# One run of narrow products for two weight units in a decoder layer

## The chip, the cores and the metric

The kernel runs on one core of a Trainium2 chip. The metric is the time of one execution on the device in microseconds (us). Three runs of the kernel before gave 642.34, 642.52 and 642.67 us; the median is 642.52.

## The reference

A decoder layer for 256 positions of width 1024, all in float32: a SwiGLU half step, a mixer of causal attention (8 heads of 128) and a short gated convolution, and a second SwiGLU half step, each followed by a layer norm.

```python
def swiglu(x, w_up, w_down):
    gate, up = jnp.split(x @ w_up, 2, axis=-1)
    return (jax.nn.silu(gate) * up) @ w_down

# one layer
x = layer_norm(ALPHA * x + 0.5 * swiglu(x, ffn1_w_up, ffn1_w_down), ln1_g, ln1_b)
z = x @ w_in                                  # (256, 8192): q, k, v, h, g_b, g_c, gates
mix = (gate_attn * (attention(q, k, v) @ w_proj_attn)
       + gate_conv * ((g_b * short_conv(g_c * h)) @ w_proj_conv)) @ w_out
x = layer_norm(ALPHA * x + mix, ln2_g, ln2_b)
x = layer_norm(ALPHA * x + 0.5 * swiglu(x, ffn2_w_up, ffn2_w_down), ln3_g, ln3_b)
```

With 256 positions the attention has a single block of keys, so it is plain causal attention. The width of the ffns is 2816.

## The kernel before

**Products.** Each float32 matrix is split into a high half, rounded to the matmul's format, and a low half, what the rounding left. A product of two matrices is high by high, high by low and low by high; low by low is left out. Weights come from memory in units of 1 MB (`Unit`, line 40): ScalarE casts a unit's `raw` buffer into the high half (tile `S`, line 895), VectorE subtracts it from the raw values into the low half (tile `LC`, or `LR` for units read by rows, line 898), in two chunks a unit (`prep`, line 889). A cast of a new unit waits until a buffer is free. `S` has five, `LC` three and `raw` three buffers; in part of the mixer two of the `S` buffers and both of `LR` hold queries and keys.

**Columns and rows.** Where the result is wanted transposed, the weights are stationary (`cols`, line 356). A unit of 1024 x 256 weights gives two blocks of 128 output columns, each with an accumulator (tile `acc`, one of eight banks). For each block and each of the eight slices `k` of the input (KT is 8) there is one *wide* product, the high weights by both halves of the input (tile `X`, 512 columns), and one *narrow* product, the low weights by the high input (256 columns). So a unit has 16 wide and 16 narrow products. A block whose last product is issued is evacuated by its epilogue, which begins with a ScalarE copy (line 386) and a VectorE addition (line 387). The order is set by hand at line 383: nine wide products, that is the eight of the first block and one of the second; the sixteen narrow ones of both blocks; the other seven wide ones. In a sequence of units the seven and the nine of the next unit form sixteen wide ones. Where the input is stationary (`rows`, `rows_both`, and `D` for the down projection), all products are 512 wide.

**Stages.** `ffn` (line 390) goes over eleven groups `j` of 256 hidden columns. The first one or two groups go by rows; each later one is `U_cols(j)`: a unit of gate weights, then one of up weights. Behind it comes `D` for group `j - 2`, 24 products for both halves of the positions, whose four accumulators stay in use until the end of the ffn. The mixer computes the values by rows, and then 14 times four blocks with `four` (line 550): q, k, q, k, the gates, h, gc, gb, each with two units. Projections `P` (line 765) do the same four times, and `O` ends the mixer by rows. In all there are 74 units with stationary weights.

**What sets the order.** TensorE's sequence is the list `base`, built in the order above. Other steps (transposes, attention's products, softmax) are put into it at planned times: `put(at, dt, ops)` inserts them `dt` us behind place `at` by a clock that counts columns / 2400 + 0.0025 us a product (line 851). A head's scores, transposes and value products are put at 1.3, 11.8 and 16.3 us behind the first keys, 7.5 us further for each head (line 747). A final loop goes over the sequence and issues everything (line 933): ahead of each product `advance` (line 910) issues what is due, loads on SyncE's queue (line 884) as raw buffers come free, casts as `S` and low buffers come free and at least 2.2 us apart, in the order in which units are first used (lines 867 to 875). A unit's buffers are given back with its last product (lines 937 to 941). The sixteen sigmoids of the gates go to ScalarE 0.6 us apart behind the first `H` (line 751).

Of the kernel before, what the change touches and what calls it, by code (L numbers as in the profile page):

```python
# [19 lines left out]
KT = DM // 128  # L20
# [45 lines left out]
def layer(ctx: ExitStack, tc: tile.TileContext, a: dict, out: bass.AP):  # L66
# [53 lines left out]
    def mm(dst, lhsT, rhs, start, stop, cols, unit=None):  # L120
        return Op(lambda: nc.tensor.matmul(dst(), lhsT=lhsT(), rhs=rhs(), start=start, stop=stop), cols, unit)  # L121

    def passes(dst, sta, mov, first, last, cols, unit=None):

        return [mm(dst, lambda x=x: sta(x), lambda w=w: mov(w), first and i == 0, last and i == 2, cols, unit)
                for i, (x, w) in enumerate(((0, 0), (0, 1), (1, 0)))]

    def add(ops):
        base.extend(ops)
        return len(base)  # L130
# [5 lines left out]
    def defer(dt, fn, unit=None):  # L136
        pending.append((now["t"] + dt, unit, fn))
# [7 lines left out]
    def new_unit(src, chunks=2, use="rows"):  # L145
        u = Unit(src, chunks, use)
        units.append(u)
        return u
# [37 lines left out]
    def col_unit(w, c0):  # L186

        return new_unit(lambda raw: [(raw.rearrange("p (k n) -> p k n", k=KT),
                                      w[:, c0:c0 + 256].rearrange("(k p) n -> p k n", p=128))], use="cols")
# [24 lines left out]
    def split_later(hi, lo, src, done=None, dt=0.8):  # L214
        def rest():
            nc.vector.tensor_tensor(lo, src, hi.bitcast(F), op=OP.subtract)
            if done:
                done()

        def first():  # L220
            nc.scalar.copy(hi, src)  # L221
            defer(0.5, rest)

        defer(dt, first)
# [128 lines left out]
            add([ops[i]])  # L353
        return len(base)

    def cols(key, u, epis):

        box, wide, narrow = {}, [], []
        for b in range(2):
            for k in range(KT):
                c = slice(k * 256 + b * 128, k * 256 + (b + 1) * 128)
                wide.append(mm(lambda b=b: box[b], lambda c=c: u.hi[:, c],
                               lambda k=k: st["xT", key][:, k].rearrange("p s t n -> p (s t n)"),
                               k == 0, b == 1 and k == KT - 1, 512, u))
                narrow.append(mm(lambda b=b: box[b][:, 0:256], lambda c=c: u.lo[:, c],
                                 lambda k=k: st["xT", key][:, k, 0].rearrange("p t n -> p (t n)"),  # L370
                                 False, b == 0 and k == KT - 1, 256, u))
        for b, end in ((0, narrow[KT - 1]), (1, wide[-1])):
            def first(b=b, f0=wide[b * KT].fn):
                box[b] = ACC.get()
                f0()

            def fin(b=b):
                epis[b](box[b])
                ACC.free()

            wide[b * KT].fn = first
            end.after.append(fin)
        return add(wide[:KT + 1] + narrow + wide[KT + 1:])

    def both(dst, bank):
        nc.scalar.copy(dst, bank[:, 256:512])  # L386
        nc.vector.tensor_tensor(dst, dst, bank[:, 0:256], op=OP.add)  # L387


    def ffn(key, wu, wd, ln_i, by_rows, order, tail, after_ln):  # L390
# [4 lines left out]
        def hT_of(j, kk):  # L395
            if ("hT", key, j, kk) not in st:
                st["hT", key, j, kk] = T.get(R).rearrange("p (s n) -> p s n", s=2)
            return st["hT", key, j, kk]
# [27 lines left out]
        def U_cols(j):  # L426
            ug, uu = col_unit(wu, j * 256), col_unit(wu, DFF + j * 256)

            def gate(bank, b):
                g = T.get()  # L430
                both(g[:, 0:256], bank)
                defer(0.8, lambda: nc.scalar.activation(g[:, 0:256], g[:, 0:256], AF.Silu))  # L432
                st["g", j, b] = g

            def up(bank, b):
                g = st["g", j, b]
                both(g[:, 256:512], bank)
                nc.vector.tensor_tensor(g[:, 0:256], g[:, 0:256], g[:, 256:512], op=OP.mult)  # L438
                hT = hT_of(j, b)
                split_later(hT[:, 0], hT[:, 1], g[:, 0:256], T.free, 1.1)  # L440

            cols(key, ug, [lambda bank, b=b: gate(bank, b) for b in range(2)])
            cols(key, uu, [lambda bank, b=b: up(bank, b) for b in range(2)])
            if j == NJ - 1:
                base[-1].after.append(X.free)

# [52 lines left out]
        for j in js:  # L499
            U_cols(j)  # L500
            while done <= j - 2:
                D([done], 0)
                if done < NJ - tail:
                    D([done], 1)
                done += 1
        e0 = D(list(range(done, NJ)), 0)
        last = list(range(NJ - tail, NJ))
# [27 lines left out]
    win = a["w_in"][0]  # L535
    COLS = {"q": 0, "k": 1024, "v": 2048, "h": 3072, "gb": 4096, "gc": 5120, "ga": 6144, "gv": 7168}

    def V(c, t):
        if ("v", c) not in st:
            st["v", c] = row_units(win, COLS["v"] + c * 512)  # L540

        def epi(bank):
            if c == 0 and t == 0:
                st["v"] = X.get(R).rearrange("p (s t n) -> p s t n", s=2, t=2)
            cs = slice(c * 512, (c + 1) * 512)
            split(st["v"][:, 0, t, cs], st["v"][:, 1, t, cs], bank)

        return rows("m", t, st["v", c], epi)

    def four(kind, c, epi):  # L550

        for p in range(2):
            u = col_unit(win, COLS[kind] + c * 512 + p * 256)
            e = cols("m", u, [lambda bank, j=p * 2 + b: epi(bank, j) for b in range(2)])
        return e

    def QK(kind, c):
        def epi(bank, j):
            if j == 0:
                state["hold" + kind] -= 1  # L560
                pool = st["pool", kind, c] = S if kind == "q" else L["rows"]
                st[kind, c] = pool.get(R).rearrange("p (s h n) -> p s h n", s=2, h=4)
            t_ = T.get()
            both(t_[:, 0:256], bank)
            split_later(st[kind, c][:, 0, j], st[kind, c][:, 1, j], t_[:, 0:256], T.free)

        return four(kind, c, epi)

    def H(c):
        def epi(bank, j):  # L570
            if j == 0:
                st["h", c] = N.get()
            both(st["h", c][:, j * 256:(j + 1) * 256], bank)

        return four("h", c, epi)

    def GC(c):
        def epi(bank, j):
            if j == 0:
                st["u", c] = N.get().rearrange("p (j n) -> p j n", j=4)  # L580
                nc.gpsimd.memset(st["u", c][:, :, 0:2], 0.0)
            u, hc, ch = st["u", c][:, j], st["h", c][:, j * 256:(j + 1) * 256], c * 4 + j
            t_ = T.get()
            both(t_[:, 0:256], bank)
            nc.vector.tensor_tensor(u[:, 2:258], t_[:, 0:256], hc, op=OP.mult)
            T.free()

            def tap2():
                nc.scalar.activation(hc, u[:, 2:258], AF.Identity, bias=cvec[:, 24 + ch:25 + ch], scale=cvec[:, 16 + ch:17 + ch])

            def taps():
                for s in (1, 0):
                    nc.vector.scalar_tensor_tensor(hc, u[:, s:s + 256], cvec[:, s * 8 + ch:s * 8 + ch + 1],
                                                   hc, op0=OP.mult, op1=OP.add)
                if j == 3:
                    N.free()

            defer(1.0, tap2)
            defer(2.6, taps)

        return four("gc", c, epi)
# [118 lines left out]
    for t in range(2):  # L720
        for c in range(2):
            e = V(c, t)
# [17 lines left out]
    for c in range(2):  # L740
        QK("q", c)
        e = QK("k", c)
# [20 lines left out]


    def P(key, w, n, epi):
        for p in range(2):
            u = col_unit(w, n * 512 + p * 256)
            cols(key, u, [lambda bank, j=p * 2 + b: epi(bank, j) for b in range(2)])

    def A_epi(n):  # L770
        def epi(bank, j):
# [22 lines left out]
    for n in range(2):  # L794
        P("a", a["w_proj_attn"][0], n, A_epi(n))
        if n == 1:
            base[-1].after.append(X.free)
        P("c", a["w_proj_conv"][0], n, C_epi(n))
# [170 lines left out]
```

## Time and profile before

| | |
|---|---|
| median of three runs | 642.52 us |
| profiled execution | 642.42 us |
| its span, first to last instruction | 640.5 us |
| TensorE's products | 3416, busy 631.6 us |
| TensorE's weight loads | 3416, busy 545.3 us |
| VectorE | busy 454.3 us |
| ScalarE | busy 355.2 us |
[...]

The profile names engines PE (TensorE's products), PEld (its weight loads), DVE (VectorE), ACT (ScalarE), POOL and SP. Products overlap each other in the array, so one product's duration is longer than the distance between two starts; the distance is read from the timeline, in which neighbours of one kind are merged into a row with the start of the first one and their number. A row's own length ends with the end of the last product, so a run's time is the start of the next row less its own start. Products read `acc<-X,S` (wide, stationary weights), `acc<-X,LC` (narrow, stationary weights), `acc<-S,T` and `acc<-LR,T` (down projection).

### The profile page before, as it was taken

What the parts mean: (1) busy time and instruction counts of PE and PEld (TensorE: products, weight loads), DVE (VectorE), ACT (ScalarE), POOL (GpSimd) and SP (SyncE); (2) the same over time, 40 slices, a digit from 0 to 9 for tenths busy, and PEclk for the clock granted to TensorE, in tenths of its full rate; (3) what the DMA queues carried; (4) which work ended last, traced back from release to release, by engine and by line L of the source; (5) the groups of instructions that cost most, each with busy time, mean ns of one, the idle gap of its engine ahead of it and who ended that gap; (6) DMA issues with size and microseconds to landing.
All of it is one profiled execution on the core that took longest, in us unless ns stands there. A gap on an engine that the chain in (4) does not pass through costs nothing.

```text
span 640.5 us, 8790 instructions
## 1 busy us (share of the span) xinstructions
PE 631.6 (99%) x3416; PEld 545.3 (85%) x3416; DVE 454.3 (71%) x732; ACT 355.2 (55%) x624; POOL 19.3 (3%) x25
## 2 busy tenths in 40 slices
PE   9999999999999999999999999999999999999995
PEld 6888888888888888898888888888888888888884
DVE  4786666666677678778768987889966666666637
ACT  5765555555533567677678664553555555555530
POOL 2000000000011000000000000001100000000001
PEclk9999999999999999999999999999999999999999
DMA  8766666557654475454646665576555755555401
GB/s 296 262 231 200 215 235 197 185 183 251 214 163 131 138 227 162 148 181 132 196 138 199 201 210 175 197 236 225 196 197 200 259 195 185 184 188 189 178 1 67
DMA packets 95854, 121.18 MB, mean 189 GB/s; under 512 B 2196, under 2 KB 84548, under 8 KB 95812
## 3 DMA queue, kind: packets, MB, share of 16 engines
q1 hardware_dynamic: 95524, 120.23, 57.2%
q8 instruction: 27, 0.44, 0.3%
q10 hardware_dynamic: 288, 0.39, 0.2%
q14 instruction: 15, 0.12, 0.1%
HBM read 119.56 MB, written 1.05 MB: 188 GB/s over the span
## 4 chain that ended last, share of the span: by engine, by line
PE 98%; DVE 1%; issue 0%; DVEq 0%; ACT 0%; POOL 0%; POOLq 0%
PE acc L121 96%; PE acc L198 2%; PE acc L155 0%; DVE N L835 0%; DVEq L965 0%; DVE LR L898 0%; DVE N L839 0%; ACT X L211 0%; POOL T L94 0%; DVE bn L248 0%; DVE N L246 0%; DVE mv L258 0%; PE acc L730 0%; DVE X L212 0%; DVEq L898 0%
## 5 line engine op out<-in xcount | busy, mean ns | idle before, releaser
L121 PE MATMUL acc<-X,S 128*128 128x512 f32 x1184 | 288.8, 392 | 0.0
L121 PEld LDWEIGHTS acc<-X,S 128*128 128x128 f32 x1184 | 216.5, 188 | 41.3
L895 ACT CAST S<-raw 128x1024 fp32r<-128x1024 f32 (+1 forms) x224 | 225.9, 1033 | 18.6 <-PE acc L121 14.4
L898 DVE TENSOR_TENSOR LC<-raw,S 128x1024 fp32r<-128x1024 f32 x166 | 201.7, 1224 | 24.9 <-ACT S L895 23.2
L121 PEld LDWEIGHTS acc<-X,LC 128*128 128x128 f32 x1184 | 149.8, 189 | 5.6
L121 PE MATMUL acc<-X,LC 128*128 128x256 f32 x1184 | 152.4, 281 | 0.0
L387 DVE TENSOR_TENSOR T<-T,acc 128x256 f32<-128x256 f32 x132 | 55.3, 419 | 97.3 <-ACT T L386 97.2
L121 PE MATMUL acc<-S,T 128*128 128x512 f32 (+1 forms) x364 | 112.1, 383 | 0.0
L386 ACT COPY T<-acc 128x256 f32<-128x256 f32 x132 | 48.9, 370 | 110.9 <-PE acc L121 110.7
L121 PEld LDWEIGHTS acc<-S,T 128*128 128x128 f32 x364 | 67.5, 188 | 13.3
L898 DVE TENSOR_TENSOR LR<-raw,S 128x1024 fp32r<-128x1024 f32 (+1 forms) x58 | 66.1, 1147 | 8.2 <-ACT S L895 8.1
L121 PE MATMUL acc<-S,X 128*128 128x512 f32 x224 | 71.6, 395 | 0.0
L121 PE MATMUL acc<-LR,T 128*128 128x512 f32 (+1 forms) x164 | 63.1, 385 | 0.0
L121 PEld LDWEIGHTS acc<-S,X 128*128 128x128 f32 x224 | 42.0, 188 | 9.5 <-ACT S L895 0.6
L121 PEld LDWEIGHTS acc<-LR,T 128*128 128x128 f32 x164 | 30.8, 188 | 6.1
L221 ACT CAST T<-T 128x256 fp32r<-128x256 f32 x38 | 15.5, 407 | 33.7 <-DVE T L438 33.7
L211 ACT CAST X<-acc 128x512 fp32r<-128x512 f32 x16 | 9.4, 586 | 26.9 <-PE acc L198 16.1
L432 ACT ACTIVATE T<-T 128x256 f32<-128x256 f32 x38 | 15.9, 418 | 14.3 <-DVE T L387 14.3
L121 PE MATMUL acc<-LC,X 128*128 128x512 f32 x56 | 22.6, 403 | 0.0
L121 PE MATMUL acc<-LR,X 128*128 128x512 f32 x56 | 22.0, 392 | 0.3 <-DVE LR L898 0.3
L212 DVE TENSOR_TENSOR X<-acc,X 128x512 fp32r<-128x512 f32 x16 | 11.0, 690 | 15.2 <-ACT X L211 15.0
L260 POOL TENSOR_TENSOR rs<-mv,mhalf 128x1 f32<-128x1 f32 x6 | 6.2, 1038 | 457.9 <-DVE mv L258 457.9
(83 smaller groups left out, 319.9 us busy)
## 6 DMA issues: line engine op xcount, KB each, us to landing
raw<-in_ffn_w_up SPq DMA_DIRECT2D x38, 1024.0 KB, 5.1
raw<-in_w_in SPq DMA_DIRECT2D x32, 1024.0 KB, 5.4
raw<-in_ffn_w_down SPq DMA_DIRECT2D x22, 1024.0 KB, 5.0
raw<-in_w_proj_attn SPq DMA_DIRECT2D x4, 1024.0 KB, 5.0
raw<-in_w_proj_conv SPq DMA_DIRECT2D x4, 1024.0 KB, 5.0
raw<-in_w_out SPq DMA_DIRECT2D x4, 1024.0 KB, 5.0
raw<-in_ffn_w_up SPq DMA_DIRECT2D x8, 512.0 KB, 5.1
raw<-in_ffn_w_up SPq DMA_DIRECT2D x8, 256.0 KB, 5.6
```

The costliest lines, as they stand in the source:

```text
L121: return Op(lambda: nc.tensor.matmul(dst(), lhsT=lhsT(), rhs=rhs(), start=start, stop=stop), cols, unit)
L198: nc.tensor.transpose(box["t"][:, i * 128:(i + 1) * 128], src(i), ident)
L211: nc.scalar.copy(hi, src)
L212: nc.vector.tensor_tensor(lo, src, hi.bitcast(F), op=OP.subtract)
L221: nc.scalar.copy(hi, src)
L260: nc.gpsimd.tensor_tensor(rs, mv[:, 1:2], mhalf, op=OP.pow)
L386: nc.scalar.copy(dst, bank[:, 256:512])
L387: nc.vector.tensor_tensor(dst, dst, bank[:, 0:256], op=OP.add)
L432: defer(0.8, lambda: nc.scalar.activation(g[:, 0:256], g[:, 0:256], AF.Silu))
L895: nc.scalar.copy(u.hi[:, s], u.raw[:, s])
L898: nc.vector.tensor_tensor(u.lo[:, s], u.raw[:, s], u.hi[:, s].bitcast(F), op=OP.subtract)
```

## The change

`cols` takes a list of units. With two of them it issues 25 wide products (all of the first unit's sixteen, eight of the second's first block and one of its second), then the 32 narrow ones of all four blocks, then the seven wide ones that are left. The epilogues of the first three blocks follow the last narrow product of each, that of the fourth the last wide one. `U_cols`, `four` and `P` hand over their two units together. The first group by columns of the first ffn (`j == by_rows`) stays as two single units. Nothing else is changed.

```diff
-    def cols(key, u, epis):
+    def cols(key, uns, epis):
         box, wide, narrow = {}, [], []
-        for b in range(2):
+        last = 2 * len(uns) - 1
+        for b in range(last + 1):
+            u = uns[b // 2]
             for k in range(KT):
-                c = slice(k * 256 + b * 128, k * 256 + (b + 1) * 128)
-                wide.append(mm(lambda b=b: box[b], lambda c=c: u.hi[:, c],
+                c = slice(k * 256 + b % 2 * 128, k * 256 + (b % 2 + 1) * 128)
+                wide.append(mm(lambda b=b: box[b], lambda c=c, u=u: u.hi[:, c],
                                lambda k=k: st["xT", key][:, k].rearrange("p s t n -> p (s t n)"),
-                               k == 0, b == 1 and k == KT - 1, 512, u))
-                narrow.append(mm(lambda b=b: box[b][:, 0:256], lambda c=c: u.lo[:, c],
+                               k == 0, b == last and k == KT - 1, 512, u))
+                narrow.append(mm(lambda b=b: box[b][:, 0:256], lambda c=c, u=u: u.lo[:, c],
                                  lambda k=k: st["xT", key][:, k, 0].rearrange("p t n -> p (t n)"),
-                                 False, b == 0 and k == KT - 1, 256, u))
-        for b, end in ((0, narrow[KT - 1]), (1, wide[-1])):
+                                 False, b < last and k == KT - 1, 256, u))
+        for b in range(last + 1):
...
-            end.after.append(fin)
-        return add(wide[:KT + 1] + narrow + wide[KT + 1:])
+            (wide[-1] if b == last else narrow[(b + 1) * KT - 1]).after.append(fin)
+        n = last * KT + 1
+        return add(wide[:n] + narrow + wide[n:])
...
-            cols(key, ug, [lambda bank, b=b: gate(bank, b) for b in range(2)])
-            cols(key, uu, [lambda bank, b=b: up(bank, b) for b in range(2)])
+            epis = [lambda bank, f=f, b=b: f(bank, b) for f in (gate, up) for b in range(2)]
+            if key == "x" and j == by_rows:
+                cols(key, [ug], epis[:2])
+                cols(key, [uu], epis[2:])
+            else:
+                cols(key, [ug, uu], epis)
...
-        for p in range(2):
-            u = col_unit(win, COLS[kind] + c * 512 + p * 256)
-            e = cols("m", u, [lambda bank, j=p * 2 + b: epi(bank, j) for b in range(2)])
-        return e
+        uns = [col_unit(win, COLS[kind] + c * 512 + p * 256) for p in range(2)]
+        return cols("m", uns, [lambda bank, j=j: epi(bank, j) for j in range(4)])
...
-        for p in range(2):
-            u = col_unit(w, n * 512 + p * 256)
-            cols(key, u, [lambda bank, j=p * 2 + b: epi(bank, j) for b in range(2)])
+        uns = [col_unit(w, n * 512 + p * 256) for p in range(2)]
+        cols(key, uns, [lambda bank, j=j: epi(bank, j) for j in range(4)])
```

## Rows read from the trace of the kernel before

**Rows 1.** The page's part 1: busy us (share of the span) xinstructions of each engine.

```profile
PE 631.6 (99%) x3416; PEld 545.3 (85%) x3416; DVE 454.3 (71%) x732; ACT 355.2 (55%) x624; POOL 19.3 (3%) x25
```

**Rows 2.** The page's part 4: the chain that ended last, by engine.

```profile
PE 98%; DVE 1%; issue 0%; DVEq 0%; ACT 0%; POOL 0%; POOLq 0%
```

**Rows 3.** Waits of the weight loads: us in total, times, longest us.

```profile
PEld acc L121 <- ACT S L895: 0.6, 1, 0.6
```

**Rows 4.** Groups of instructions: shapes xcount | busy us, mean ns | idle before.

```profile
L121 PE MATMUL acc<-X,S 128*128 128x512 f32 x1184 | 288.8, 392 | 0.0
L121 PEld LDWEIGHTS acc<-X,S 128*128 128x128 f32 x1184 | 216.5, 188 | 41.3
L121 PE MATMUL acc<-X,LC 128*128 128x256 f32 x1184 | 152.4, 281 | 0.0
L387 DVE TENSOR_TENSOR T<-T,acc 128x256 f32<-128x256 f32 x132 | 55.3, 419 | 97.3 <-ACT T L386 97.2
```

**Rows 5.** Timeline of PE, first ffn, one period (start us, us, ...).

```profile
80.36 2.20 PE L121 MATMUL acc<-X,S 128*128 128x512 f32 x9
82.40 2.05 PE L121 MATMUL acc<-X,LC 128*128 128x256 f32 x16
84.28 3.82 PE L121 MATMUL acc<-X,S 128*128 128x512 f32 x16
87.94 2.05 PE L121 MATMUL acc<-X,LC 128*128 128x256 f32 x16
89.83 1.78 PE L121 MATMUL acc<-X,S 128*128 128x512 f32 x7
91.44 0.39 PE L121 MATMUL acc<-S,T 128*128 128x512 f32 x1
...
96.88 0.62 PE L121 MATMUL acc<-X,S 128*128 128x512 f32 x2
```

**Rows 6.** Timeline of PE, first ffn: first rows of two periods, six apart.

```profile
63.84 2.20 PE L121 MATMUL acc<-X,S 128*128 128x512 f32 x9
...
162.96 2.20 PE L121 MATMUL acc<-X,S 128*128 128x512 f32 x9
```

**Rows 7.** Timeline of PE, mixer: a run of six narrow products.

```profile
266.56 0.87 PE L121 MATMUL acc<-X,LC 128*128 128x256 f32 x6
267.27 2.69 PE L121 MATMUL acc<-X,S 128*128 128x512 f32 x11
269.80 0.49 PE L198 MATMUL acc<-ident,T 128*128 128x128 f32 x3
```

**Rows 8.** Timeline of all engines, first ffn: a narrow run's loads and products.

```profile
104.24 2.06 PEld L121 LDWEIGHTS acc<-X,LC 128*128 128x128 f32 x16
104.46 2.05 PE L121 MATMUL acc<-X,LC 128*128 128x256 f32 x16
```

**Rows 9.** Timeline of PE, mixer: a narrow run behind an attention step.

```profile
304.64 1.98 PE L121 MATMUL acc<-X,LC 128*128 128x256 f32 x16
306.45 1.56 PE L121 MATMUL acc<-X,S 128*128 128x512 f32 x6
```

**Rows 10.** Timeline of PE, mixer: the rest of a narrow run behind three transposes.

```profile
298.59 1.40 PE L121 MATMUL acc<-X,LC 128*128 128x256 f32 x10
299.82 3.82 PE L121 MATMUL acc<-X,S 128*128 128x512 f32 x16
```

**Rows 11.** Timelines of PE and ACT, mixer, while the sigmoids run: a release, two casts.

```profile
330.43 3.81 PE L121 MATMUL acc<-X,S 128*128 128x512 f32 x16
...
335.57 1.04 ACT L895 CAST S<-raw 128x1024 fp32r<-128x1024 f32 x1
...
338.21 1.04 ACT L895 CAST S<-raw 128x1024 fp32r<-128x1024 f32 x1
```

**Rows 12.** DMA issues: KB each, median us from issue to landing.

```profile
raw<-in_w_in SPq DMA_DIRECT2D x32, 1024.0 KB, 5.4
```

**Rows 13.** Windows 251:318, 318:337 and 337:348 summed: us, then each engine's busy us.

```profile
sum 97.00, PE 97.00 PEld 86.28 DVE 74.28 ACT 71.67 POOL 0.11; mean PE 32.33 PEld 28.76 DVE 24.76 ACT 23.89 POOL 0.04
```

## The prediction

> **What bounds the kernel now.** I read the page's engine list first, then the chain, then the waits of TensorE, then its products in order of time. TensorE is busy 99% of the span, the next engine 71% [rows 1], and 98% of the chain that ended last is TensorE [rows 2]. Its loads waited three times for a weight in the whole span, 0.6 us at the longest [rows 3]. So no wait is left to remove: the time is the number of products times the distance from one start to the next. Busy times (392 and 281 ns for one product, [rows 4]) don't give that distance, because products overlap; I take it from the starts in the timeline.
>
> One ffn pair of units shows it [rows 5]. The first nine wide products go from 80.36 to 82.40, 2.04 us or 226.7 ns each. Sixteen narrow ones follow in 1.88 us, 117.7 ns each. Then sixteen wide ones take from 84.28 to 87.94, 3.66 us, where sixteen at 226.7 ns would take 3.63; the seven after the second narrow run take 1.61 us against 1.59. The 24 products of the down projection are back at 226.7 ns (91.44 to 96.88, 5.44 us). So wide products behind a narrow run start slow and recover: each return from narrow to wide costs about 30 ns; the step from wide to narrow costs nothing that I can see. Six such periods, from 63.84 to 162.96 [rows 6], take 99.12 us, 16.52 each; 56 wide ones at 226.7 and 32 narrow ones at 117.7 ns would be 16.46. The 0.06 us left belong to two narrow runs: **30 ns a run**, now at a resolution of a few ns.
>
> **What the change removes.** There are 1184 wide and 1184 narrow products with stationary weights [rows 4], 16 of each in a unit: 74 units, 37 pairs. The first pair of the first ffn stays as it is, 36 pairs are merged, and each loses one narrow run. 36 x 0.030 = **1.1 us**. Products, loads and columns stay the same in number, and so do all instructions of the other engines and all DMAs.
>
> Does a run of 32 return to wide products more dearly than one of 16? A run of only six narrow ones (266.56 to 267.27) is followed by eleven wide ones in 2.53 us, 0.03 over eleven at 226.7 [rows 7]: the same 30 ns as behind sixteen. The cost is one of the return, not of the run's length, so I take 30 ns behind 32 too. The bounds are 60 ns, twice the cost behind twice the run, which leaves a gain of nothing, and 0, which would make it 36 x 0.060 = 2.2 us; [rows 7] speak for the middle.
>
> Is the second half of a longer run as fast as the first? The loads of a narrow run start at 104.24 and take 2.06 us, its products start at 104.46 and take 2.05 [rows 8]: the loads stay one product ahead from first to last, and no reserve is being used up. [...] A bound on the other side: where an attention step broke the rhythm, sixteen narrow ones took from 304.64 to 306.45, 1.81 us, 113 ns each [rows 9]. If the second half of each long run fell into that rhythm, 36 x 16 x 0.0045 = 2.6 us more would be gained. Nothing in the sixteen places of an undisturbed run moves that way, so I take 117.7.
>
> **What it moves.** Attention steps are put at planned times in the sequence and now meet other products. A step's three transposes cost the run that they break little: the ten narrow products behind them take 1.23 us where 1.18 is due [rows 10]; other steps leave the faster rhythm of [rows 9] behind, 0.07 us a run the other way. By the planner's own clock two of the eight fall into narrow runs, about as now. I count 0 and +-0.2 us.
>
> The epilogues of three of the four blocks come 8 narrow products apart (0.94 us) after the change, no longer spread over the pair; the last stays at the pair's end. Four accumulators are open instead of two. In the ffns the down projection holds four more, so all eight are in use, but its 24 products (5.44 us, [rows 5]) stand between two pairs and cover the last epilogue, an addition of 0.42 us [rows 4] behind a copy. In the mixer the other four are free. Cost 0; without that cover a pair would wait about 0.8 us, an estimate that takes the copy to be as long as the addition.
>
> The weights are held longer. Now a unit's buffers come free 5.54 us after its first product; after the change the first unit's come free behind 25 wide and 16 narrow ones, 25 x 0.2267 + 16 x 0.1177 = 7.55 us into the pair, the second's at its end, 11.05. With three buffers for low halves the first unit of the next pair is cast from the start of this pair and gains time. The second one is cast from 7.55 us on, and its first wide product is due at 11.05 + 16 x 0.2267 + 0.03 = 14.7: **7.15 us** instead of two units, 11.1. Where ScalarE is free its two casts, planned 2.2 us apart, have room; where it is late it is close. The latest I find is among the sigmoids: the unit released at about 332.0 (seven products into the run of 330.43) was followed by casts at 335.57 and 338.21 to 339.25, 7.25 us [rows 11]. That would be 0.1 us too late after the change, but the second cast is needed only four wide products later, 0.9 us: 0.8 us is left. DMA issues on SyncE keep their order and move with the releases; a load needs 5.4 us [rows 12], and its raw buffer is free from the cast three units earlier, over a pair's 11 us ahead. The low halves are needed later than now, behind 25 or more wide products, which covers VectorE's lag.
>
> **The sum.** The profiled execution took 642.42 us, its span 640.5; the median of the runs is 642.52, so a difference of the span carries over. 642.5 - 1.1 = **641.4**, 640.5 - 1.1 = 639.4 for the span.
>
> **Rivals.**
> - *No gain* (642.5): the 30 ns are no price of the return, but follow the number of narrow products before it, or come back elsewhere. For it: the excess is small beside the rounding of one row. Against it: six periods agree, and six narrow ones cost as much as sixteen [rows 6, 7]. [...]
> - *A wait for weights at one or two places* (641.6 to 642.5): the second unit of a pair comes late behind the sixteen sigmoids of ScalarE, near 335 to 341, where 0.8 us is left. Each us beyond that is one us of TensorE, once.
> - *Slower* (646 to 647): the same wait over the whole stretch from 251 to 348, where ScalarE is busy 71.7 of 97 us [rows 13]. It decides from the point where ScalarE is over 4.3 us late to a release (3.5 is the worst here). About nine pairs lie there; at 5 us late each loses 0.7, 6 us in all, less the 1.1 gained: 647. Against it: in that stretch epilogues and casts are the same work, only in other bursts.
> - *More gain* (638.8): the faster rhythm of [rows 9] in the second halves.
>
> **How the numbers follow.** Forecast 641.4 +-0.3: 0.66. Wait at one or two places 0.10, no gain 0.09, slower 0.07, more gain 0.08. What a measurement can tell is about 0.2%, 1.28 us: the forecast of 1.1 lies just inside it, and a third of its 0.66, for the steps that are moved and for the bound of the return, lies beyond, 0.22. Faster 0.22 + 0.08 = 0.30; same 0.44 + 0.10 + 0.09 = 0.63; slower 0.07. The range runs from 640.3, where the return is free behind 32 (2.2 us), to 642.7; it takes in the forecast, the single wait and no gain, and leaves out 0.15.
>
> **What would show it.** In the ffns of the changed kernel a period should be 25 wide ones in 5.67 us, 32 narrow ones in 3.77 without a step at the seventeenth, seven wide ones in 1.61, and 16.49 us in all against 16.52. The wide run in the middle of the pair must show no slow start. The rows of waits of TensorE's loads should hold no new entry for ScalarE's casts; one near 341 would be the single wait, entries at each pair from 251 on the slower case. Casts of a pair should come as two and two, the second pair of casts some 7.6 us into it. I am wrong if the seven wide ones behind 32 take over 1.64 us, if narrow ones drift, or if loads wait.

## The result and the profile after

The changed kernel takes 648.2 us (648.07 to 648.97) beside 642.55 us for the kernel before: a ratio of 1.0091, 95% interval 1.0079 to 1.0103. It is 5.6 us slower where 1.1 us less was forecast, and it lies outside the range. The execution profiled took 648.07 us, its span is 646.3 us against 640.5 us, so the 5.8 us can be looked for in the trace.

The page's engine list and its chain by engine, after:

```profile
PE 633.1 (98%) x3416; PEld 544.5 (84%) x3416; DVE 452.3 (70%) x732; ACT 351.1 (54%) x624; POOL 19.9 (3%) x25
PE 86%; DVE 9%; ACT 4%; issue 1%; DVEq 0%; POOL 0%; ACTq 0%; POOLq 0%
```

The engine list hardly differs from [rows 1]: the instructions are the same in number, and VectorE and ScalarE are even a little less busy. The share of TensorE falls by one point, too little to draw the eye. The chain is what changed: 98% TensorE in [rows 2], now 86%, with 13% on VectorE and ScalarE. The waits of the weight loads say at what it stands (engine, line, what is waited for: us in total, times, longest us):

```profile
PEld acc L121 <- DVE T L212: 3.5, 5, 2.2
PEld acc L121 <- DVE LR L902: 2.4, 3, 1.2
PEld acc L121 <- DVE LC L902: 2.0, 2, 1.2
...
PEld acc L121 <- ACT X L221: 0.7, 1, 0.7
PEld acc L121 <- ACT S L899: 0.6, 1, 0.6
```

The wait for ScalarE's cast is what it was (0.6 us, [rows 3]). New is the wait for the attention's transposed probabilities (`T`, line 212), and so is one for the input of `O` (`X`, line 221). The waits for low halves of weights (`LR` and `LC`, line 902) have grown: in the kernel before there was one of each, 0.6 and 0.3 us. What is new lies in two stretches. In the windows of the kernel after, then of the kernel before (length in us, busy us and number of instructions of each engine, granted clock, DMA share, GB/s), 225 to 310 us is queries, keys and the first attention steps, 425 to 475 us the end of the mixer and the first rows of the second ffn:

```profile
225.00:310.00 85.00, 83.00 (x492) 72.44 (x491) 64.32 (x145) 57.07 (x131) 0.00 (x0) 1.00 0.49 149
...
425.00:475.00 50.00, 47.45 (x221) 37.72 (x221) 42.39 (x64) 24.00 (x36) 6.04 (x4) 1.00 0.61 202
```

```profile
225.00:310.00 85.00, 85.00 (x514) 75.50 (x513) 67.34 (x155) 59.00 (x138) 0.00 (x0) 1.00 0.57 171
...
425.00:475.00 50.00, 50.00 (x231) 40.76 (x230) 41.59 (x61) 25.15 (x37) 6.04 (x4) 1.00 0.66 215
```

TensorE issues 22 products fewer in the one and ten fewer in the other, at a granted clock of 1.00 in both kernels (over the whole span 0.998 before, 0.996 after): it is not the clock. No engine is busier there than before, but for VectorE in the second window, by 0.8 us. What is lost is lost by waiting.

For the place to a few hundredths of a us I take the start of each stage's first product from TensorE's timeline (inside a merged row by its place in the row) and compare stage lengths with those of the kernel before. The columns of the table: the attention part is from the second queries (`q1`) to `gc0`, eight pairs, then `O`, then the rows of the second ffn's first group, and the rest are the stages in which only the length of undisturbed work can change. The rows below the first belong to the experiments. (The rest of m_mid and of v_c0a1c1 holds 0.3 us that lie ahead of the first merged pair, where the program is the same.)

| kernel | attention part | `O` | first rows of ffn 2 | all the rest | span |
|---|---|---|---|---|---|
| after | +3.10 | +2.1 | +1.6 | -1.1 | +5.8 |
| e_hold | +1.6 | +1.4 | +1.6 | +0.1 | +4.7 |
| e_late | +1.6 | -0.2 | 0.0 | 0.0 | +1.4 |
| e_both | +1.1 | 0.0 | +1.6 | +0.1 | +2.8 |
| e_ffn | 0.0 | 0.0 | 0.0 | -0.7 | -0.7 |
| m_tail | +3.1 | 0.0 | +1.6 | -1.1 | +3.6 |
| m_attn | +1.8 | +2.1 | +1.6 | -1.2 | +4.3 |
| m_mid | +1.7 | -0.1 | +1.6 | -1.4 | +1.9 |
| m_at2 | +0.1 | +2.1 | +1.6 | -1.2 | +2.7 |
| b_at2 | +0.2 | 0.0 | 0.0 | 0.0 | +0.2 |
| b_cast77 | 0.0 | 0.0 | +1.6 | 0.0 | +1.7 |
| v_c0a1c1 | +0.1 | 0.0 | 0.0 | -1.3 | -1.2 |
| v_p21 | +0.1 | +1.1 | 0.0 | -1.1 | +0.1 |

So the gain that was forecast is there, -1.1 us outside the disturbed stages, and three losses stand against it: 3.1 + 2.1 + 1.6 = 6.8 us. The 2.1 us of `O` are two things: 0.6 in its first quarter, the wait for its own input (`X`), and 1.5 in its second, waits for low halves.

**The gain.** The same period of the first ffn as in [rows 5] (start us, us, engine, line, what), and, from the view of all engines, the weight loads of its narrow run:

```profile
80.25 5.83 PE L121 MATMUL acc<-X,S 128*128 128x512 f32 x25
85.69 3.95 PEld L121 LDWEIGHTS acc<-X,LC 128*128 128x128 f32 x32
85.92 3.93 PE L121 MATMUL acc<-X,LC 128*128 128x256 f32 x32
89.69 1.77 PE L121 MATMUL acc<-X,S 128*128 128x512 f32 x7
91.30 0.39 PE L121 MATMUL acc<-S,T 128*128 128x512 f32 x1
...
96.74 0.62 PE L121 MATMUL acc<-X,S 128*128 128x512 f32 x2
```

25 wide products in 5.67 us (226.8 ns each, no slow start in the middle), 32 narrow ones in 3.77 (117.8 ns), seven wide ones in 1.61, the period 16.49 us against 16.52. All four are the forecast's numbers. The loads of the 32 take 3.95 us, their products 3.93 us: they stay one product ahead from first to last.

**Where the attention's loss shows first.** ScalarE, at the first keys' pair of units (`k0`; last bracket: idle before, and what ended it):

```profile
228.26 1.05 ACT L899 CAST S<-raw 128x1024 fp32r<-128x1024 f32 x1
232.35 0.37 ACT L389 COPY T<-acc 128x256 f32<-128x256 f32 x1 [3.04 <-PE acc L121]
```

The copy is the first step of the pair's first epilogue. It used to be due behind nine wide and eight narrow products, now it is due behind 25 and eight: 16 x 0.2267 = 3.6 us later (in the traces it starts at 229.17 us before and at 232.35 after). ScalarE stands 3.04 us, and then three epilogues fall due 0.94 us apart (their copies start at 232.35, 233.52 and 235.04 us). From this instant on the chain that ended last has no piece of TensorE for 55 us, only ScalarE and VectorE (start us, us, what; the pieces between are casts, copies, subtractions and softmax steps):

```profile
214.43 17.89 PE acc L121 x97
...
232.35 0.38 ACT T L389
...
286.72 0.30 DVE T L212
287.06 4.30 PE acc L121 x27
```

TensorE feels it first at the second head's value products. After, then before:

```profile
259.98 0.49 PE L198 MATMUL acc<-ident,T 128*128 128x128 f32 x3
264.96 0.37 ACT L211 CAST T<-acc 128x256 fp32r<-128x256 f32 x1
266.33 0.42 DVE L212 TENSOR_TENSOR T<-acc,T 128x256 fp32r<-128x256 f32 x1
266.80 0.19 PEld L121 LDWEIGHTS acc<-T,X 128*128 128x128 f32 x1 [2.18 <-DVE T L212]
```

```profile
260.44 0.49 PE L198 MATMUL acc<-ident,T 128*128 128x128 f32 x3
262.89 0.37 ACT L211 CAST T<-acc 128x256 fp32r<-128x256 f32 x1
264.11 0.29 DVE L212 TENSOR_TENSOR T<-acc,T 128x128 fp32r<-128x128 f32 x1 [0.33 <-ACT T L211]
265.40 0.70 PE L121 MATMUL acc<-T,X 128*128 128x512 f32 x4
```

Before, ScalarE takes the transposed probabilities 2.45 us behind the transposes, and VectorE ends its second split (264.40) 1.0 us ahead of the products. After, ScalarE comes 4.98 us behind the transposes, the first split ends at 266.75, and the load behind it starts at once, at 266.80. The products had been put there by the planned clock, and TensorE starts nothing of what stands behind them in its list either: its loads stand for 2.18 us, its products for 1.75. ScalarE does nothing for 3.04 us here and 3.39 us below, each time ahead of a copy whose product was still to come.

**The end of the mixer.** ScalarE after, behind the last pairs of the projections:

```profile
417.98 2.95 ACT L899 CAST S<-raw 128x1024 fp32r<-128x1024 f32 x3
424.32 0.37 ACT L389 COPY T<-acc 128x256 f32<-128x256 f32 x1 [3.39 <-PE acc L121]
...
427.67 1.05 ACT L899 CAST S<-raw 128x1024 fp32r<-128x1024 f32 x1
...
430.65 1.05 ACT L899 CAST S<-raw 128x1024 fp32r<-128x1024 f32 x1
```

and the loads of `O`, which wait for the low halves that VectorE makes from such casts:

```profile
435.40 0.19 PEld L121 LDWEIGHTS acc<-LC,X 128*128 128x128 f32 x1 [0.83 <-DVE LC L902]
...
439.21 0.19 PEld L121 LDWEIGHTS acc<-LC,X 128*128 128x128 f32 x1 [1.19 <-DVE LC L902]
```

In units read by rows a low half is needed one product behind its high half; in the column units it has 25 wide products' time, 5.67 us in the first ffn.

**The second ffn's first rows.** ScalarE after, two casts around the layer norm:

```profile
444.84 1.05 ACT L899 CAST S<-raw 128x1024 fp32r<-128x1024 f32 x1 [5.26 <-PE acc L121]
...
451.45 1.05 ACT L899 CAST S<-raw 128x1024 fp32r<-128x1024 f32 x1
```

Before, the same instant shows two casts in a row (`x2`, shown with its experiment below). A layer norm sets a pause of 4 us by the planned clock in which no cast is issued (`QUIET`; `ln_stats`, line 255). In the program's own plan, the cast of the second ffn's first unit, second chunk (unit 77 in its order, counted from 0), is due at 405.85 us, ahead of the very product behind which the pause is set; the next place in the sequence, 0.2 us later, would be too late. (The planned clock counts less for a product than the trace shows, 0.216 us for a wide one against 0.227; the product at the pause starts at 437.2 us in the trace before and at 441.6 us after.) After the change every cast from the projections' last unit on is due about 2 us later: 382.05 instead of 380.10 for unit 72, 405.63 instead of 403.47 for the first chunk of unit 77. The second chunk misses its place and is issued behind the pause, at 409.95, and every cast behind it is one place later too. The casts shown at 444.84 and 451.45 us are, counted along that list, the two chunks of the next unit (78).

### The profile page after: what moved, and what is told of

The parts are those of the page before. It is cut to its first block, busy times and chain, and to the rows that moved or that the text cites. A ratio compares the mean times of both kernels' runs of the same rounds, so it can differ in the third digit from the quotient of the medians.

```text
span 646.3 us, 8776 instructions
## 1 busy us (share of the span) xinstructions
PE 633.1 (98%) x3416; PEld 544.5 (84%) x3416; DVE 452.3 (70%) x732; ACT 351.1 (54%) x624; POOL 19.9 (3%) x25
## 4 chain that ended last, share of the span: by engine, by line
PE 86%; DVE 9%; ACT 4%; issue 1%; DVEq 0%; POOL 0%; ACTq 0%; POOLq 0%
PE acc L121 84%; DVE LC L902 2%; PE acc L198 1%; DVE LR L902 1%; ACT S L899 1%; DVE T L390 1%; ACT T L389 0%; PE acc L155 0%; DVE T L212 0%; DVE LR L216 0%; DVE bn L248 0%; ACT X L211 0%; DVE N L791 0%; DVE N L792 0%; DVE mx L666 0%
## 5 line engine op out<-in xcount | busy, mean ns | idle before, releaser
L121 PE MATMUL acc<-X,S 128*128 128x512 f32 x1184 | 282.1, 391 | 0.0
L121 PEld LDWEIGHTS acc<-X,S 128*128 128x128 f32 x1184 | 218.6, 188 | 43.3
L902 DVE TENSOR_TENSOR LC<-raw,S 128x1024 fp32r<-128x1024 f32 x164 | 197.2, 1219 | 10.2 <-ACT S L899 10.0
L121 PEld LDWEIGHTS acc<-X,LC 128*128 128x128 f32 x1184 | 145.0, 189 | 2.9
L121 PE MATMUL acc<-X,LC 128*128 128x256 f32 x1184 | 146.6, 281 | 0.0
L121 PE MATMUL acc<-S,T 128*128 128x512 f32 (+1 forms) x364 | 112.1, 383 | 0.0
L121 PEld LDWEIGHTS acc<-S,T 128*128 128x128 f32 x364 | 67.5, 188 | 13.3
L121 PE MATMUL acc<-S,X 128*128 128x512 f32 x224 | 72.0, 396 | 0.3 <-ACT X L221 0.3
L902 DVE TENSOR_TENSOR LR<-raw,S 128x1024 fp32r<-128x1024 f32 (+1 forms) x60 | 68.0, 1166 | 1.4 <-ACT S L899 1.4
L121 PE MATMUL acc<-LR,T 128*128 128x512 f32 (+1 forms) x164 | 63.0, 384 | 0.0
L121 PEld LDWEIGHTS acc<-S,X 128*128 128x128 f32 x224 | 42.1, 188 | 10.1 <-ACT X L221 0.7
L121 PEld LDWEIGHTS acc<-LR,T 128*128 128x128 f32 x164 | 30.8, 188 | 6.1
L121 PE MATMUL acc<-LR,X 128*128 128x512 f32 x64 | 25.4, 397 | 1.1 <-DVE LR L902 1.1
L121 PE MATMUL acc<-LC,X 128*128 128x512 f32 x48 | 19.4, 405 | 1.2 <-DVE LC L902 1.2
L212 DVE TENSOR_TENSOR X<-acc,X 128x512 fp32r<-128x512 f32 x16 | 10.9, 686 | 11.4 <-ACT X L211 11.4
```

The lines of the kernel that those rows point to most:

```text
L902: nc.vector.tensor_tensor(u.lo[:, s], u.raw[:, s], u.hi[:, s].bitcast(F), op=OP.subtract)
```

## The experiments

The variants are built from the changed kernel with a set of the pairs that are merged; the other pairs run in the order of the kernel before. Lines in the variants are shifted: L127, L218 and L943 there are L121, L212 and L902 of the changed kernel. The kernel before took 642.32 to 642.35 us beside them. My theory behind the result was that the weights' later release costs the time; the rival was the bunching of the epilogues.

### One part of the change at a time, in the order of before

**e_hold.** No pair is merged; the first unit of each pair gives its buffers back as late as the merged pair does, with the ninth product of the second unit.

```diff
-            if op.unit.left == 0:
+            if op.unit.left == 0 and op.unit.mate is None:
                 S.free()
                 op.unit.pool.free()
+            for u in held:
+                if op.unit is u.mate and op.unit.left == 23:
+                    S.free()
+                    u.pool.free()
```

> The order of products of before, and its epilogues; only the buffers of a pair's first unit are given back later, behind the ninth product of the second unit (7.58 us into the pair instead of 5.54), which is when the changed kernel gives them back. In the changed kernel some 3.0 us are lost between 260 and 300 us and some 3.7 between 428 and 465, 1.1 are gained, 5.65 more in all. Theory 'hold' (casts of a pair's second unit come too late and push all later casts): the whole gross loss is here, 649.3. Theory 'burst' (epilogues of three blocks 0.94 us apart, and ScalarE's queue standing before the first of them): 642.6. If it needs both, under 645.

Measured: 646.91 us, ratio 1.0069 (1.0055 to 1.0083). **e_late** leaves the releases and issues the epilogues of the first two blocks of each pair as late as the merged pair does:

```diff
-        ends = [narrow[KT - 1], wide[2 * KT - 1], narrow[3 * KT - 1], wide[-1]]
+        ends = [wide[2 * KT + 4], wide[2 * KT + 8], narrow[3 * KT - 1], wide[-1]]
```

> The order of products of before, and its releases of buffers; only the epilogues of a pair's first two blocks are issued later, behind the fifth and the ninth wide product of the second unit (6.67 and 7.58 us into the pair), so that they come at the times of the changed kernel, 6.61 and 7.55. Theory 'burst': the whole gross loss is here, 649.3. Theory 'hold': 642.6. If it needs both, under 645.

Measured: 643.7 us, 1.0021 (1.0012 to 1.003). **e_both** does both:

> The order of products of before with the late release and the late epilogues together. If these two are all that the change does besides the 36 saved returns from narrow to wide, the time is that of the changed kernel plus 1.1: 649.3 (+-0.4), with waits at the same two places. If the order of products matters by itself, it stays clearly below, near 645.

Measured: 645.22 us, 1.0043 (1.0027 to 1.0058). The waits of the loads in e_hold, and then in e_late:

```profile
PEld acc L127 <- DVE LR L943: 2.9, 5, 1.2
PEld acc L127 <- DVE T L218: 2.0, 5, 0.6
...
PEld acc L127 <- DVE LC L943: 1.9, 2, 1.2
```

```profile
PEld acc L127 <- DVE T L218: 1.9, 5, 0.5
```

The later release alone makes a loss in all three places, without a single product changing its place. Late epilogues alone make a loss in the attention and no other. So theory and rival both have a part there: each alone costs the attention 1.6 us, and only the release costs `O` and the second ffn. The two don't add: with both, `O` loses nothing, and the whole is 1.7 us cheaper than the release alone.

e_hold and e_late came out at the time of neither theory (649.3 or 642.6 us), and e_both is 4.1 us below the 649.3 that it would need if the two were all that the change does. By its own text that speaks for the order of products mattering by itself. The two together give the whole loss of the second ffn, but 1.1 of 3.1 us in the attention and nothing of the 2.1 in `O`; no run separates what makes up the rest. The traces show one thing that these runs leave out. In the order of before, the block of a late epilogue's copy has long been finished. The copy that starts at 232.35 us in the changed kernel, after 3.04 us of standing, starts at once in e_both:

```profile
229.18 0.37 ACT L430 COPY T<-acc 128x256 f32<-128x256 f32 x1
```

So e_late and e_both move an epilogue's place in the queue, not the product that it waits for. That the standing by itself is what costs isn't shown either: from 241.20 to 261 us ScalarE's rows are the same in e_both and in the changed kernel, within 0.2 us. Then pieces stand in another order in its queue (a copy at 262.89 us ahead of the exponentials, in the changed kernel at 263.79 behind them), and it takes the transposed probabilities at 264.34 and 264.96 us. In `O`, too, the traces differ by order: e_hold casts unit 73's second chunk at 422.00 us behind epilogue steps that wait for VectorE, e_both has both chunks in a row from 416.59 ahead of them, and the second chunk of unit 75, which the second quarter of `O` needs, comes 4.4 and 3.0 us behind the start of `O`. This is read from the traces, not shown by a run of its own.

### One part of the pairs at a time

**e_ffn** merges only the eighteen pairs of the two ffns.

```diff
+MERGED = {f"x{j}" for j in range(2, 11)} | {f"f{j}" for j in range(2, 11)}
```

> The change in the two ffns alone: 18 pairs merged (nine of each ffn), the mixer as before. 18 x 0.030 = 0.54 us less than before, 642.0, by the term of the sum that was read from the trace; both theories on the loss place it in the mixer and expect the same. 642.5 or more if the return costs more behind 32 narrow products, or if the ffns lose something too.

Measured: 641.58 us (641.52 to 641.72), 0.9987 (0.9978 to 0.9996): 0.74 us, 0.041 us a pair. Against a rival of no gain this interval is decisive, just; the forecast's 0.030 a pair lies in it. All of it lies in the two ffns' columns (0.40 and 0.33 us of the table's 0.7). By the trace a merged pair's period is 0.033 us shorter. Some 0.1 us more lies behind the last pair of the first ffn, in a stretch that is 0.13 us shorter in e_hold and 0.10 in e_both, where nothing is merged; so 0.041 is too much for a return.

Three variants merge all but some of the mixer's pairs. **m_tail** leaves the projections' last two (`a1`, `c1`) single:

> The changed kernel, but the last pairs of the mixer's projections (a and c of the second half) stay single units, so the buffers that the last weights of the projections and the output's wait for come free as before. Theory: lateness of the casts begins with the later release in these pairs, and reaches TensorE in the output projection and the next ffn's first rows. Then 3.8 us of stalls between 428 and 465 go and two saved returns with them: 648.2 - 3.8 + 0.1 = 644.5, the stalls at 264 to 287 staying. Rival: the casts have been late since the attention stretch, and the last pairs are only where it is seen; then the stalls between 428 and 465 stay, 648.2.

Measured: 646.25 us, 1.0058 (1.0045 to 1.0072). **m_attn** leaves the six from `q1` to `gv1` single:

> The changed kernel, but the six pairs among which the attention steps lie (q, k of the second half, and the four of the gates) stay single. Theory: the stalls at 264 to 287 come from these pairs' own late casts and bunched epilogues, which hold up the softmax of heads 0 and 2; they go (some 3.1 us), 0.2 of gain with them: 645.3, the stalls from 428 on staying. Rival: the pairs before them (q and k of the first half) set the lateness; the stalls stay, 648.

Measured: 646.78 us, 1.0067 (1.0051 to 1.0082). **m_mid** leaves all eight single:

> The changed kernel with these eight pairs single and 28 merged. Theory: both losses are gone and 28 returns are saved; by the merged ffns 0.74 / 18 = 0.041 us a pair, so 642.3 - 28 x 0.041 = 641.2, no stall over 0.2 us on TensorE's loads beyond those of before. Rival (lateness begins elsewhere): above 643.

Measured: 644.64 us, 1.0032 (1.002 to 1.0045). All three missed by 1.5 to 3.4 us, in two places. `O`'s loss is that of the last two pairs: it goes with them. But the loss in the second ffn's first rows, which I had put to the same pairs, stays: by the plan the first chunk of unit 77 is still due at 404.34 us in m_tail and m_mid, 0.9 later than before, and the second misses its place. And the attention keeps 1.7 to 1.8 us of its 3.1 in m_attn and m_mid, although none of its first six pairs is merged: that part of the lateness is carried in from `q0` and `k0`. The waits in m_tail show the one loss gone (no `LC` row of 2.0; one of 0.3 is left, as before) and the two that stay:

```profile
PEld acc L127 <- DVE T L218: 3.5, 5, 2.1
PEld acc L127 <- DVE LR L943: 2.5, 3, 1.1
```

### The planned times

If the attention's loss is a matter of a planned time that no longer fits, a later time must remove it, with all pairs merged. **m_at2** is the changed kernel with the value products planned 2.5 us later; **b_at2** is the kernel before with the same edit, to know what it does by itself.

```diff
-OFF, AT0, AT1, AT2, HEAD = 5.0, 1.3, 10.5, 15.0, 7.5
+OFF, AT0, AT1, AT2, HEAD = 5.0, 1.3, 10.5, 17.5, 7.5
```

> The changed kernel with a head's value products planned 2.5 us later (17.5 instead of 15.0 us behind its scores). Theory 'a planned time that no longer fits': the softmax chain is late by up to 2.2 us at the value products of heads 0 and 2, and with 2.5 us more room the stalls at 264 to 287 go: 648.2 - 3.1 = 645.1. Theory 'the two engines have fallen behind for good there': the chain falls further behind, and over 1 us of stalls stays in the stretch: 646.5 or more.

> The kernel before with the attention's value products planned 2.5 us later, nothing merged: what that alone is worth, since the changed kernel with it lost nothing in the attention. There is no wait there before, so 642.3 +-0.3; a gain or a loss over 0.6 us would mean that the later place does something else than give room.

Measured: m_at2 645.15 us, 1.0043 (1.003 to 1.0057); b_at2 642.52 us, 1.0003 (0.9994 to 1.0011). m_at2 is 3.05 us below the changed kernel, as much as the attention's loss, and its wait is gone but for 0.2 us, while the other two stay (the heads that waited are the second and the fourth, not "0 and 2"):

```profile
PEld acc L127 <- DVE LR L943: 2.4, 3, 1.2
PEld acc L127 <- DVE LC L943: 2.0, 2, 1.2
...
PEld acc L127 <- DVE T L218: 0.2, 1, 0.2
```

The same edit is worth nothing in the kernel before, so it is no gain of its own. ScalarE and VectorE are not too slow for the merged pairs; they are late to a time that was fixed for the old order.

**b_cast77** takes the kernel before and only holds back the one cast that the plan has at 405.85 us until 406.0, so that it falls into the pause:

```diff
+                if state["prep"] == 77 and c == 1 and t < 406.0:
+                    break
```

> The kernel before, with nothing merged; one single cast is planned later: the second chunk of the second ffn's first unit. By the planner's clock it is due at 405.85 in the kernel before and the pause of 4.0 us behind the first half's layer norm begins at 405.95; here it may not come before 406.0, falls into the pause, and is issued at 409.95. In the changed kernel the chain of casts is 2.2 us late there and the same cast falls into the pause. Theory 'a cast chain that misses the slot ahead of the layer norm': the 1.64 us that the changed kernel loses in the second ffn's first rows come back here without any merging, 642.3 + 1.6 = 643.9, with waits for VectorE's low halves near 455 and 458. Rival: that loss needs the merged pairs' bunched work; 642.3.

Measured: 644.06 us (643.93 to 644.55), 1.0027 (1.0018 to 1.0036). ScalarE in the kernel before, and then in b_cast77:

```profile
430.63 3.89 ACT L895 CAST S<-raw 128x1024 fp32r<-128x1024 f32 x4
440.38 2.00 ACT L895 CAST S<-raw 128x1024 fp32r<-128x1024 f32 x2 [5.86 <-PE acc L121]
```

```profile
430.63 3.90 ACT L895 CAST S<-raw 128x1024 fp32r<-128x1024 f32 x4
440.42 1.06 ACT L895 CAST S<-raw 128x1024 fp32r<-128x1024 f32 x1 [5.89 <-PE acc L121]
...
447.02 1.05 ACT L895 CAST S<-raw 128x1024 fp32r<-128x1024 f32 x1
```

VectorE in the kernel before, and then in b_cast77:

```profile
449.16 1.22 DVE L898 TENSOR_TENSOR LR<-raw,S 128x1024 fp32r<-128x1024 f32 x1
```

```profile
454.68 1.22 DVE L898 TENSOR_TENSOR LR<-raw,S 128x1024 fp32r<-128x1024 f32 x1
```

and TensorE in b_cast77, and then a weight load of the changed kernel at the same place:

```profile
455.95 0.50 PE L121 MATMUL acc<-LR,X 128*128 128x512 f32 x1 [0.73 <-DVE LR L898]
...
457.93 0.50 PE L121 MATMUL acc<-LR,X 128*128 128x512 f32 x1 [0.32 <-DVE LR L898]
```

```profile
460.38 0.19 PEld L121 LDWEIGHTS acc<-LR,X 128*128 128x128 f32 x1 [1.15 <-DVE LR L902]
```

One cast that misses its place costs 1.7 us, the whole third loss, with no pair merged. The held cast itself is not late on the chip: counted along the program's list it is the last of the four from 430.63 us in both kernels, as ScalarE is ahead of the plan there. But everything behind it is issued one place later. The cast at 447.02 us is the second chunk of unit 78, 5.7 us late (about 441.3 before, the second half of the row of two). And the low half of the first chunk of unit 79 stood ahead of the second half's layer norm in VectorE's queue; now it stands behind it, 5.5 us later (449.16 and 454.68 us). TensorE's waits at 455.95 and 457.93 us are for the two low halves of that unit. All kernels bear the sign: where one cast stands at the place of the row of two (after, e_hold, e_both, m_tail, m_attn, m_mid, m_at2) the rows lose 1.6 us; where two do (before, e_late, e_ffn, b_at2, v_c0a1c1, v_p21) they lose nothing. (The 405.95 us that the expectation gives for the pause's beginning is no place in the sequence: the pause is set at 405.85, behind the product ahead of which the cast is due.)

### What is left when the causes are taken away

**v_c0a1c1** merges all but `c0`, `a1` and `c1`, the pairs whose release comes last ahead of `O`, and has `AT2` at 17.5; its planned casts from unit 72 on are those of before. **v_p21** merges all 36 pairs, has `AT2` at 17.5, and lets casts follow each other more closely, which takes the cast at issue back to 405.85:

```diff
-LEAD, LEAD0, LEAD1, PACE, DELAY, QUIET = 30.0, -1.0, 0.9, 2.2, 1.2, 4.0
+LEAD, LEAD0, LEAD1, PACE, DELAY, QUIET = 30.0, -1.0, 0.9, 2.1, 1.2, 4.0
```

> The changed kernel with the value products 2.5 us later and the last three pairs (c of the first half, a and c of the second) single: 33 pairs merged. By the planner's clock all casts from the projections' last unit on are then due exactly as before. Theory (three places, each with its own cause: planned times of the attention, the last pairs' releases, the pause behind the layer norm): all three losses are gone, 642.3 - 33 x 0.041 = 641.0. Rival (the losses come from merging itself and move elsewhere): 643 or more.

> The changed kernel, all 36 pairs merged, with the value products 2.5 us later and casts allowed 2.1 us apart instead of 2.2. By the planner's clock the last unit ahead of the first layer norm's pause is again due at 405.85, but the output projection's casts are still up to 1.7 us later than before. Theory: the 1.64 us in the ffn's first rows are gone, the attention too, and of the 2.1 us in the output projection most stay: 642.3 - 36 x 0.041 + 1.5 to 2.1 = 642.4 to 643.0. If the pace of casts was all, 640.9.

Measured: v_c0a1c1 641.51 us (641.05 to 641.97), 0.9986 (0.9977 to 0.9994); v_p21 642.49 us, 1.0001 (0.9991 to 1.001). The first beats both kernels; its chain is 98% TensorE again. By 0.033 us a pair its forecast would have been 641.2. It can't be told from e_ffn (641.58 us) by time, though it merges fifteen pairs more. v_p21 has neither the attention's nor the second ffn's loss and half of `O`'s (1.1 us, of which 0.9 in the first quarter: there it is the wait for the input of `O`, which closer casts don't cure), and that eats the gain of 36 pairs. `PACE` is a constant that concerns the whole kernel; that it helps shows that the delay of the casts is one of the plan, not that 2.1 is better by itself.

## Why the prediction was wrong

**Right: what bounds the kernel and the term of the sum.** The distances, the flat rhythm of 32 narrow products, the price that follows the return and not the run's length, the seven wide ones: each as forecast, 36 x 0.030 = 1.1 us; a return measures 0.033. Where nothing else interferes, the stages of the nine pairs of each ffn and of ten of the mixer's are 1.07 us shorter, of which some 0.1 is not the merging's. The rivals of no gain and of more gain fall with that.

**Wrong first: "The weights are held longer ... 0.8 us is left".** This is the step that failed first. It was priced within the mixer's pairs, at the wide product of the next pair's second unit that needs the cast. That product indeed never waits. But casts are one list, in order of first use, at least 2.2 us apart. A release that comes 2 us later puts off every cast behind it, and the pace gives little back. The bill comes in `O` (1.5 of its 2.1 us) and in the second ffn (1.6), whose row units need the low half one product behind the high one, without the cover that column units have. "Covers VectorE's lag" was worked out for column units only; the units behind the last pair were not looked at. e_hold shows this step by itself: +4.6 us, 3 of them in those two places.

**Wrong second: the pause.** `advance` issues what is due, and has a rule of which neither the description nor the sum took account: a stretch of 4 us that lets no cast pass. In the kernel before, one cast passes at the last product ahead of it. A step of 1.6 us hung on that margin, and b_cast77 shows that it takes no merging to fall over it.

**Wrong third: "I count 0 and +-0.2 us" for the attention, and "Cost 0" for the epilogues.** What the steps cost TensorE itself is small, as forecast: m_at2, with all pairs merged, is 0.1 us longer there. But both prices were TensorE's and the accumulators'; neither asked when ScalarE and VectorE come to the transposed probabilities, or to the input of `O` (0.6 us). The copy of the first epilogue of `k0` is due 3.6 us later, and ScalarE stands for 3.04 us ahead of it; the cast issued behind it starts at 233.79 us. The room at the second head was 1.0 us. That the epilogues' place in the queue and the release can each cost something there is shown by e_late and e_hold (+1.6 each); that the loss is the planned time and not the engines' capacity is shown by m_at2. How the 3.1 us come about when all pairs are merged stays open: the two together give 1.1 us in the order of before.

**The slower rival** had the right direction (646 to 647 us; 648.2 measured) and the wrong place: it looked for waits for ScalarE's casts from 251 to 348 us, pair by pair, and none is there. The chance of 0.07 rested on comparing ScalarE's work with the room in single pairs; what decided was order and planned time, in which a margin of one product counts.

**Left open:** what the merged order adds to the release and the late epilogues, 2.0 us in the attention and 2.1 in `O` (the changed kernel against e_both), and, but for what the traces show of the queues, why late epilogues spare `O` the loss that late releases cause (e_both against e_hold).

## What to carry to other kernels

A regrouping of products that saves some nanoseconds each also moves the moments at which buffers come free and results are due; in a kernel with hand-set times, follow every release and every epilogue to the next thing of the same queue, beyond the stage that is changed, and list the margins against fixed times (here 1.0 us at a value product and a single product's place at a pause) before the gain is counted. Where the chain of waits leaves the bounding engine while all busy shares stay as they were, look for a planned time that no longer fits, and test it by moving that time alone in both kernels. Merge where nothing hangs on the timing (the ffns gave 0.7 us), and move the neighbouring constants together with the order where something does.

## What the runs showed of the hardware

Not expected: of 5.8 us lost, only 4.3 show as idle time of TensorE in the engine list (646.3 - 633.1 against 640.5 - 631.6); the same 3416 products are busy 1.5 us more. Busy time counts a moment once (1184 wide products of 392 ns each would be 464 us, their group is busy 288.8, [rows 4]), and beside this wait products overlap less: the four value products at 266.80 us, with a second wait among them, take 1.19 us where their row in the kernel before took 0.70, and from their start to the next product TensorE is busy 0.90 of 1.03 us, before 0.53 of 0.53. And the delays of two changes don't add: +4.6 us (later releases) and +1.4 us (later epilogues) alone, +2.9 us together.
